# Attention scores by 64-row tiles, carried in PSUM from chunk to chunk, in turns of two chunks

## The chip, the core and the metric

The kernel runs on one core of a Trainium2 chip. TensorE multiplies matrices into PSUM, VectorE (DVE in the profile), ScalarE (ACT) and GpSimd (POOL) work on tiles, and SyncE (SP) issues the transfers between HBM and SBUF. The metric is device microseconds of one execution. Before the change three runs took 1882.86, 1883.38 and 1887.03 us, median 1883.38.

## The reference

One encoder layer runs on two sequences, "prompt" with 1024 tokens and "sample" with 2048, all in float32, 1024 channels wide. What matters here, cut from the reference:

```python
def hybrid_layer(x, mem, ...):
    h = rms_norm(x, norm_pre)
    z = jnp.einsum('btd,de->bte', h, w_in)
    u_pool, g_pool, q, k, v, g_attn, q_x, g_x = jnp.split(z, SPLITS, axis=-1)
    pool_out = multiscale_pool(u_pool, pool_w, pool_scale) * jax.nn.silu(g_pool)
    q = apply_rope(rms_norm(q.reshape(B, T, N_HEADS, HEAD_DIM), q_norm), cos, sin)
    k = apply_rope(rms_norm(k.reshape(B, T, N_KV_HEADS, HEAD_DIM), k_norm), cos, sin)
    attn_out = block_self_attention(q, k, v) * jax.nn.silu(g_attn)
    x_out = memory_attention(q_x, k_m, v_m) * jax.nn.silu(g_x)
    mix = jnp.concatenate([pool_out, attn_out, x_out], axis=-1)
    y = jnp.einsum('bte,ed->btd', mix, w_out)
    return x + rms_norm(y, norm_post)
```

Self-attention has 8 query heads of 64 dimensions and 2 key heads, so 4 query heads share one key head; it is not causal. Cross-attention has 4 heads over 256 memory tokens. Both are a softmax of scaled scores times values.

## The kernel before

**First stage.** The memory tokens, then blocks of 512 tokens, are normalised, transposed and multiplied by slices of `w_in`. For accuracy a float32 operand is split into a high part that the fast matmul format holds (`F32R`) and the rest, the low part (`split`), and a product is three matmuls: high by high, high by low, low by high. Queries and keys get norm and rotary positions, are transposed by TensorE (`heads_transposed`), split, and stored in HBM scratch: `DQ` and `DK` for self-attention, `DQX` and `DKM` for cross-attention, `DG` for the gates, `DV` for the values.

**Attention loop.** The queries are taken in pairs of two 128-query blocks (`Pair`, 256 queries; 8 pairs of the sample, then 4 of the prompt). A pair has three `Group`s: kind 0 and 1 are the two key heads with their four query heads, so 2 × 512 columns of queries; kind 2 is cross-attention. That makes 36 groups. A group runs over chunks of 128 keys: 16 in the sample, 8 in the prompt, 2 in cross-attention, 344 chunks in all.

The scores of a chunk stand with keys on the partitions. In `weights` two matmuls make them for each half `j` of the queries: `KA` has the high and the low part of the keys on its 128 partitions and meets the high part of the queries twice (`qa`); `KB` has the high part again and a 65th row of ones, and meets the low part of the queries and a 65th row with the negated maximum (`qb`). ScalarE takes the exponential of 512 columns from PSUM into `P`. `sums` adds the `P` of all chunks into `z`; in the sample VectorE adds one half and GpSimd the other (`CUT`), in the prompt VectorE adds all. `values` multiplies `P` by `V` in plain float32, two heads side by side in 64 columns of the array each, four chunks at a time (`RUN`). `totals` sums `z` over the keys, `inverse` takes the reciprocal and spreads it over 64 rows by way of HBM (`rows`, `gz`), `take` multiplies by the gate, and `mix_out` with `store_mix` multiplies by the inverse total and splits the result into `mix`.

The negated maximum comes from a look ahead: `largest` computes scores with queries on the partitions into a tile `N` of 1024 columns (two matmuls, two tiles in turn), and VectorE reduces it to one number per query. After a group's last look `shift` transposes these numbers and writes them to the row of `qb` in four small transfers.

**The order of work.** TensorE, ScalarE, VectorE and GpSimd run in the order in which the program is written; the transfers of SP are placed by the planner. The loop has one slot per chunk; work that belongs to a later slot is put in a list with `at` and issued by `due`. In a slot come the scores of half 0, the sums of the chunk before, one look, due work, the scores of half 1, pieces of the output projection (`piece`, three matmuls of 512 columns each) of an earlier pair, and work due at the half slot (`END`), where the values stand. `looks` is filled backward so that a group's last look stands at least `LEAD` = 4 slots ahead of its first. 20 looks are done beside the last matmuls of the first stage (`look_ahead`). PSUM in the loop holds two tiles `N` (two banks each), two `S` (one bank), `acc` and `py`.

## Time and profile before

| | |
|---|---|
| runs | 1882.86, 1883.38, 1887.03 us |
| profiled execution: span from first to last instruction | 1878.7 us |
| its own time outside the span | not recorded; the median of the runs is 4.7 us above the span |
| TensorE clock granted, mean | 0.994 |
| first scores of the loop, last values | 699.1 us, 1837.7 us |

The profile is one execution. Its busy time of TensorE counts overlapping matmuls once, and their modelled ends reach past the start of the next one, so the cost of a matmul is better read from the distance of two starts. In the lines of groups the shape `128*64` of a matmul is rows by columns of the weights, then comes rows by columns of what streams past; behind the bar stand the busy time, the mean in ns, and the idle time before with what ended it. `N`, `S`, `acc`, `py` are the tiles named above.

### The profile page before, as it was taken

The numbers are of one execution on the slowest core, as the hardware profiler recorded it, in microseconds if no ns is written. First come the engines' busy times: TensorE is split into PE (matmuls) and PEld (weight loads), VectorE is DVE, ScalarE is ACT, GpSimd is POOL, SyncE is SP. The second block draws the span as 40 slices with busy tenths as digits, with TensorE's granted clock in tenths as the row PEclk, the third lists the DMA queues.
The fourth block names the chain that finished last, engine by engine and source line by source line (L and its number), as shares of the span: only waits on it lengthen the run. The fifth ranks groups of instructions, "written<-read, shape, count | busy, mean of one in ns | idle before, by whom it ended". The sixth has DMA issues, their size and how long they took to land. (4 is left out here: it accounts for less than half of the span.)

```text
span 1878.7 us, 23531 instructions
## 1 busy us (share of the span) xinstructions
PE 1813.4 (97%) x8520; PEld 1279.4 (68%) x8520; DVE 1135.6 (60%) x1312; ACT 696.8 (37%) x1266; POOL 846.5 (45%) x748
## 2 busy tenths in 40 slices
PE   7999999999999999999999999999999999999997
PEld 6888888988988884465564656556465655565564
DVE  7745145431544168867768576776858576757744
ACT  5523234222422115444435344443434343333331
POOL 3655016520446007845638374563837452413311
PEclk9999999999999999999999999999999999999998
DMA  7634454254434926212122221212222153223211
GB/s 244 201 113 120 108 162 132 73 154 116 121 99 114 216 65 173 73 27 79 48 79 62 68 62 29 80 45 79 63 68 63 51 137 78 96 85 96 87 43 62
DMA packets 148485, 181.83 MB, mean 97 GB/s; under 512 B 21504, under 2 KB 118416, under 8 KB 148368
## 3 DMA queue, kind: packets, MB, share of 16 engines
q1 hardware_dynamic: 148368, 180.33, 33.9%
q8 instruction: 67, 1.10, 0.3%
q14 instruction: 50, 0.41, 0.1%
HBM read 126.50 MB, written 53.62 MB: 96 GB/s over the span
## 5 line engine op out<-in xcount | busy, mean ns | idle before, releaser
L227 ACT ACTIVATE P<-S 128x512 f32<-128x512 f32 x688 | 399.3, 598 | 555.5 <-PE S L220 430.8
L194 DVE TENSOR_REDUCE nb<-N 128x1 f32<-128x1024 f32 x256 | 311.7, 1218 | 239.8 <-PE N L191 239.0
L239 POOL TENSOR_TENSOR z<-z,P 128x512 f32<-128x512 f32 x224 | 318.4, 1421 | 222.5 <-ACT P L227 217.4
L252 PE MATMUL acc<-P,V 128*64 128x512 f32 (+1 forms) x1472 | 319.4, 576 | 0.5
L220 PE MATMUL S<-qa,KA 128*128 128x512 f32 x640 | 274.6, 429 | 9.7 <-ACT P L227 9.7
L63 POOL TENSOR_TENSOR rs<-rs,mhalf 128x1 f32<-128x1 f32 (+2 forms) x100 | 101.0, 1013 | 401.8 <-DVE rs L61 401.8
L240 DVE TENSOR_TENSOR z<-z,P 128x512 f32<-128x512 f32 (+1 forms) x272 | 271.0, 996 | 13.1 <-ACT P L227 12.9
L220 PE MATMUL S<-qb,KB 65*128 65x512 f32 x640 | 254.0, 397 | 0.0
L550 PE MATMUL pz<-hT_hi,w_hi 128*128 128x512 f32 x592 | 233.1, 394 | 1.3 <-ACT vmst L808 0.8
L552 PE MATMUL pz<-hT_hi,w_lo 128*128 128x512 f32 x592 | 232.1, 392 | 0.5 <-DVE w_lo L69 0.5
L551 PE MATMUL pz<-hT_lo,w_hi 128*128 128x512 f32 x592 | 232.3, 392 | 0.0
L191 PE MATMUL N<-KA,qa 128*128 128x512 f32 x640 | 207.5, 405 | 17.9 <-DVE rz L272 11.2
L252 PEld LDWEIGHTS acc<-P,V 128*64 128x64 f32 x1472 | 98.3, 138 | 178.7 <-issue 169.6
L220 PEld LDWEIGHTS S<-qa,KA 128*128 128x128 f32 x640 | 120.4, 188 | 143.9 <-issue 72.6
L194 DVE TENSOR_REDUCE top<-N 128x1 f32<-128x1024 f32 (+1 forms) x88 | 107.0, 1219 | 94.3 <-PE N L191 74.5
L191 PEld LDWEIGHTS N<-KA,qa 128*128 128x128 f32 x640 | 116.6, 191 | 60.9 <-DVE nb L194 21.9
L550 PE MATMUL pz<-w_hi,hT_hi 128*128 128x384 f32 (+1 forms) x416 | 140.2, 338 | 0.9 <-ACT hT_hi L68 0.8
L551 PE MATMUL pz<-w_lo,hT_hi 128*128 128x384 f32 (+1 forms) x416 | 139.4, 335 | 0.8 <-DVE w_lo L69 0.8
L552 PE MATMUL pz<-w_hi,hT_lo 128*128 128x384 f32 (+1 forms) x416 | 139.7, 338 | 0.0
L359 PE MATMUL py<-wo_hi,mix 128*128 128x512 f32 x352 | 137.7, 391 | 0.0
L360 PE MATMUL py<-wo_lo,mix 128*128 128x512 f32 x352 | 137.7, 391 | 0.0
L361 PE MATMUL py<-wo_hi,mix 128*128 128x512 f32 x352 | 137.4, 390 | 0.0
(120 smaller groups left out, 2479.5 us busy)
## 6 DMA issues: line engine op xcount, KB each, us to landing
wraw<-w_in SPq DMA_DIRECT2D x15, 1536.0 KB
dg<-gst SPq DMA_DIRECT2D x48, 256.0 KB
qa<-dq SPq DMA_DIRECT2D x48, 256.0 KB
gz<-rows SPq DMA_DIRECT2D x72, 128.0 KB
x<-x_sample SPq DMA_DIRECT2D x16, 512.0 KB
xr<-x_sample SPq DMA_DIRECT2D x16, 512.0 KB
y_sample<-xr SPq DMA_DIRECT2D x16, 512.0 KB
dq<-qst SPq DMA_DIRECT2D x96, 64.0 KB
```

Source lines behind the costliest of these rows:

```text
L191: nc.tensor.matmul(S[:, 512 * b:512 * b + 512], lhsT=q, rhs=KA[self.kind][:, k:k + 512], start=True, stop=True)
L194: nc.vector.tensor_reduce(out=out, in_=S, axis=AX.X, op=ALU.max, negate=True)
L220: nc.tensor.matmul(S, lhsT=K[self.kind][rows_, keys], rhs=q, start=n == 0, stop=n == 1)
L227: nc.scalar.activation(out=self.P[k][:, j], in_=S, func=AF.Exp)
L239: nc.gpsimd.tensor_tensor(out=z[:, :cut], in0=a[:, :cut], in1=P[:, :cut], op=ALU.add)
L240: nc.vector.tensor_tensor(out=z[:, cut:], in0=a[:, cut:], in1=P[:, cut:], op=ALU.add)
L252: nc.tensor.matmul(self.acc[64 * j:64 * j + 64, x], lhsT=v, rhs=P[:, j, x], start=(k, i) == (0, 0), stop=k == self.chunks - 1, skip_group_ ...
L359: nc.tensor.matmul(ps, lhsT=mh, rhs=wo_hi[:, c, cols], start=first, stop=False)
L360: nc.tensor.matmul(ps, lhsT=mh, rhs=wo_lo[:, c, cols], start=False, stop=False)
L550: nc.tensor.matmul(ps, lhsT=sh, rhs=mh, start=c == 0, stop=False)
L551: nc.tensor.matmul(ps, lhsT=sh, rhs=ml, start=False, stop=False)
L552: nc.tensor.matmul(ps, lhsT=sl, rhs=mh, start=False, stop=c == n - 1)
```

## The change

**Scores.** Keys and queries are laid out so that one half of the query heads has partitions 0 to 63 and the other 64 to 127. A matmul now contracts over 64 rows and the two halves stand side by side, each into its own PSUM bank of an `S` tile of 1024 columns. Two `S` tiles are used in turn, and a chunk's scores are not started afresh: the first two chunks of a group begin with a matmul of ones by a tile that holds the negated maxima (`rows`), and every chunk adds the product of the queries with the difference between its keys and those two chunks earlier. The first stage makes these differences and stores their high and low part (`DH`, `DL`), and the high part of the keys themselves for the looks (`KH`). Three products are added: high difference by high query, high by low, low by high. Cross-attention has keys of its own in both chunks and no carrying. The exponential takes 1024 columns at once.

**Looks.** A look covers 512 keys for two heads of 128 queries, by 64 rows, with the high part of the keys alone. It uses one tile `N` in the loop instead of two. The maxima of the parts are joined by a reduction; the shift goes out in eight small transfers, four for each half.

**Turns.** The loop advances by turns of two chunks: a look, the scores of both, a look, then totals and inverse of a finished group, projection, and the values of the turn before. `LEAD` is one turn.

**Rest.** `totals` uses the bank of `acc`. `inverse` transposes the totals, takes 8 reciprocals per row and spreads and transposes them back. The gate tile takes the gated product, with four buffers. The splits into `mix` are due when the tile `mix` of the pair before is free (`pair.free`), apart from the multiplication that makes their input. `P` has five buffers instead of six.

```diff
-    DK = [scratch(f"dk{s}", [2, 2, 64, T]) for s, (_, T) in enumerate(SEQS)]
+    DK = [scratch(f"dk{s}", [2, 3, 64, T]) for s, (_, T) in enumerate(SEQS)]
...
-        for a in range(0, SEQS[s][1], 1024):
-            nc.sync.dma_start(out=t[kind][h:h + 64, a:a + 1024].bitcast(F32), in_=DK[s][kind][hl, :, a:a + 1024])
+        for h in range(2):
+            for a in range(0, SEQS[s][1], 1024):
+                nc.sync.dma_start(out=tiles[kind][64 * h:64 * h + 64, a:a + 1024].bitcast(F32),
+                                  in_=DK[s][kind][which, :, a:a + 1024])
...
-            self.parts = 1 if kind == 2 else T // 1024
+            self.parts = 1 if kind == 2 else T // 512
             self.pieces = [(0, j) for j in range(2)] if kind == 2 else \
-                [(a, lane) for a in range(self.parts) for lane in range(8)]
-            self.P = {}
+                [(a, lane) for a in range(self.parts) for lane in range(4)]
+            self.P, self.S = {}, {}
...
-            self.gate = dbl.tile([128, 2, 2, 128], F32, name="gate", tag="gate")
+            self.gate = dbl.tile([128, 2, 2, 128], F32, name="gate", tag="gate", bufs=4)
...
-                q = self.qa[:, lane // 4, 128 * (lane % 4):128 * (lane % 4) + 128]
-                for b in range(2):
-                    k = 1024 * a + 512 * b
-                    nc.tensor.matmul(S[:, 512 * b:512 * b + 512], lhsT=q,
-                                     rhs=KA[self.kind][:, k:k + 512], start=True, stop=True)
-                out = self.nb[:, a, lane:lane + 1] if self.parts > 1 else self.top[:, lane:lane + 1]
+                for j in range(2):
+                    h = slice(64 * j, 64 * j + 64)
+                    nc.tensor.matmul(S[:, 512 * j:512 * j + 512],
+                                     lhsT=self.q[h, 0, 128 * lane:128 * lane + 128],
+                                     rhs=KH[self.kind][h, 512 * a:512 * a + 512], start=True, stop=True)
+                S = S.rearrange("p (j k) -> p j k", j=2)
+                out = self.nb[:, a].rearrange("p (j i) -> p j i", j=2)[:, :, lane]
...
             if self.parts > 1:
-                nc.vector.tensor_tensor(out=self.top[:, 0:8], in0=self.nb[:, 0], in1=self.nb[:, 1],
-                                        op=ALU.min)
-            self.qb = early.tile([128, 2, 512], F32R, name="qb", tag="qb", bufs=3)
-            load_K(self.s, self.kind, KB, 0, 0)
-            self.load_q(self.qb[0:64], 1)
+                nc.vector.tensor_reduce(out=self.top[:, 0:8], in_=self.nb.rearrange("p a i -> p i a"),
+                                        axis=AX.X, op=ALU.min)
+                load_K(self.s, self.kind, DH, 1)
+                load_K(self.s, self.kind, DL, 2)
             r = lanes_to_rows(self.top, "top")
-            row = self.qb[64:65].rearrange("o j (l b r) -> o (j l) b r", b=4, r=32)
-            for b in range(4):
-                nc.sync.dma_start(out=row[:, :, b].bitcast(F32), in_=r[32 * b:32 * b + 8])
-
-
-        def weights(self, k, j):
-            if j == 0:
-                self.P[k] = dbl.tile([128, 2, 512], F32, name="P", tag="P", bufs=6)
-            S = pss.tile([128, 512], F32, name="S", tag="S")
+            for j in range(2):
+                row = self.rows[64 * j:64 * j + 1].rearrange("o (i b r) -> o i b r", b=4, r=32)
+                for b in range(4):
+                    nc.sync.dma_start(out=row[:, :, b].bitcast(F32), in_=r[32 * b + 4 * j:32 * b + 4 * j + 4])
+
+
+        def weights(self, k):
+            self.P[k] = dbl.tile([128, 2, 512], F32, name="P", tag="P", bufs=PBUFS)
+            halves = [(slice(64 * j, 64 * j + 64), 512 * j) for j in range(2)]
             keys = slice(128 * k, 128 * k + 128)
-            for n, (K, q) in enumerate(((KA, self.qa[:, j]), (KB, self.qb[0:65, j]))):
-                rows_ = slice(0, 128 if n == 0 else 65)
-                if self.kind < 2:
-                    nc.tensor.matmul(S, lhsT=K[self.kind][rows_, keys], rhs=q, start=n == 0, stop=n == 1)
-                    continue
-                for i in range(2):
-                    x = slice(256 * i, 256 * i + 256)
-                    nc.tensor.matmul(S[:, x], lhsT=K[2][rows_, i, j, keys], rhs=q[:, x],
-                                     start=(n, i) == (0, 0), stop=(n, i) == (1, 1),
-                                     skip_group_check=True)
-            nc.scalar.activation(out=self.P[k][:, j], in_=S, func=AF.Exp)
+            if k < 2:
+                self.S[k] = pss.tile([128, 1024], F32, name="S", tag="S")
+                for h, at in halves:
+                    nc.tensor.matmul(self.S[k][:, at:at + 512], lhsT=ones_r[h], rhs=self.rows[h],
+                                     start=True, stop=False, skip_group_check=True)
+            S = self.S[k % 2]
+            for n, (kx, qx) in enumerate(((0, 0), (0, 1), (1, 0))):
+                for i in range(2 if self.kind == 2 else 1):
+                    x, w = (256 * i, 256) if self.kind == 2 else (0, 512)
+                    for h, at in halves:
+                        K = K2[0][h, i, kx, keys] if self.kind == 2 else (DH, DL)[kx][self.kind][h, keys]
+                        nc.tensor.matmul(S[:, at + x:at + x + w], lhsT=K, rhs=self.q[h, qx, x:x + w],
+                                         start=False, stop=n == 2, skip_group_check=True)
+            nc.scalar.activation(out=self.P[k].rearrange("p j q -> p (j q)"), in_=S, func=AF.Exp)
...
-            self.zt = psn.tile([128, 1024], F32, name="N", tag="N")
+            self.zt = psa.tile([128, 512], F32, name="acc", tag="acc")
...
-            self.o = dbl.tile([128, 512], F32, name="o", tag="o")
-            nc.vector.tensor_tensor(out=self.o, in0=self.acc,
-                                    in1=self.gate.rearrange("p i t q -> p (i t q)"), op=ALU.mult)
+            self.o = self.gate.rearrange("p i t q -> p (i t q)")
+            nc.vector.tensor_tensor(out=self.o, in0=self.acc, in1=self.o, op=ALU.mult)
 
         def inverse(self):
 
-            r = dbl.tile([128, 256], F32, name="rz", tag="rz", bufs=1)
-            nc.vector.reciprocal(out=r, in_=self.zt[:, 0:256])
+            r = dbl.tile([128, 8, 32], F32, name="rz", tag="rz", bufs=1)
+            nc.vector.transpose(out=r.rearrange("p b r -> p (b r)"), in_=self.zt[:, 0:256])
+            one = dbl.tile([128, 8], F32, name="ro", tag="ro", bufs=1)
+            nc.vector.reciprocal(out=one, in_=r[:, :, 0])
+            nc.vector.tensor_copy(out=r, in_=one.unsqueeze(2).broadcast_to([128, 8, 32]))
+            self.gz = dbl.tile([128, 512], F32, name="gz", tag="gz")
+            back = self.gz[:, 0:256]
+            nc.vector.transpose(out=back, in_=r.rearrange("p b r -> p (b r)"))
             rows = dram.tile([4, 256], F32, name="rows", tag="rows", bufs=4)
-            nc.sync.dma_start(out=rows, in_=r[0:128:32])
-            self.gz = dbl.tile([128, 512], F32, name="gz", tag="gz")
+            nc.sync.dma_start(out=rows, in_=back[0:128:32])
...
-        hi, lo = [m[:, c:c + 2] for m in pair.mix]
-
         e = nc.vector if pair.last else nc.gpsimd
         e.tensor_tensor(out=a, in0=a, in1=b, op=ALU.mult)
-        at(slot + 1 + END, nc.scalar.copy, hi, a)
-        at(slot + 2, e.tensor_tensor, lo, a, hi.bitcast(F32), ALU.subtract)
+
+        def high():
+            nc.scalar.copy(out=pair.parts()[0][:, c:c + 2], in_=a)
+
+        def low():
+            hi, lo = [m[:, c:c + 2] for m in pair.parts()]
+            e.tensor_tensor(out=lo, in0=a, in1=hi.bitcast(F32), op=ALU.subtract)
+
+        free = max(slot, pair.free)
+        at(free + 0.4, high)
+        at(free + 0.6, low)
...
-    HOLD = (16, 26)
-    LEAD, RUN = 4, 4
+    HOLD = (12, 21)
+    LEAD, PBUFS = 1, 5
...
+        pair.free = 6 if pair is pairs[0] else first[pair.groups[0]] + HOLD[pair.s]
+        at(min(ends) + 2, pair.pool, min(ends) + 2)
         for g in pair.groups:
...
+            wait = first[g] + g.chunks // 2 + 2
+            at(wait + 0.6, g.mix_out, wait + 1, pair)
+        at(max(max(ends) + 5, pair.free + 1), open_fill, pair, max(max(ends) + 5, pair.free + 1))
+    value_runs, sums_at = {}, {}
     for g in groups:
...
+        n, c = first[g], g.chunks // 2
+        at(n + 0.2, g.load_late)
+        for k in range(c):
+            value_runs[n + k + 1] = g, [2 * k, 2 * k + 1]
+        at(n + c + 0.6, g.take)
+        sums_at[n + c + 1] = g
...
+        for _ in range(2):
+            able = [g for g in groups if left[g] and first[g] - LEAD > n]
+            if able:
+                looks.setdefault(n, []).insert(0, (able[0], left[able[0]].pop()))
...
+            if k == 0:
+                loads.setdefault(max(n - 2, -1), []).append(g)
...
+            if keys is not None:
+                old = steps[keys % 2]
+                d = pt[:, 1]
+                if keys > 1:
+                    d = ftwo.tile([128, 128], F32, name="kstep", tag="kstep")
+                    nc.vector.tensor_tensor(out=d, in0=pt[:, 1], in1=old, op=ALU.subtract)
+                split(o[:, 0, 2], o[:, 1, 2], d)
+                nc.scalar.copy(out=old, in_=pt[:, 1])
...
-                    store_heads(o, 1, DK[s][j][:, :, 128 * tt:128 * tt + 128], j)
+                    store_heads(o, 0, DQ[s, tt // 2, 1][j, :, :, tt % 2, 1], j)
+                    store_heads(o, 2, DK[s][j][1:3, :, keys].rearrange("x d t -> d x t"), j)
+                    nc.sync.dma_start(out=DK[s][j][0, :, keys], in_=o[64 * j:64 * j + 64, 0, 1].bitcast(F32))
...
+    psn = pool("psn2", 1, PSUM)
...
+        n = -(-len(fill) // max(1, until[0] - turn)) if fill else 0
+        for _ in range(n):
+            out, h, c, start, final = fill.pop(0)
+            out.piece(h, c, start, final)
...
+            for x in loads.get(turn, ()):
+                x.load()
+            due(turn)
+            look(turn)
+            if before:
+                before.sums(kb + 1)
+            due(turn + 0.2)
             if g:
...
+                g.weights(k)
+                g.weights(k + 1)
+            look(turn)
+            if turn in sums_at:
+                sums_at[turn].totals()
+                sums_at[turn].inverse()
             if g:
...
+                g.sums(k)
+            due(turn + 0.4)
+            pieces = project(turn)
+            if turn in sums_at or (fill and until[0] > turn):
+                next(pieces)
+            if turn in value_runs:
+                h, ks = value_runs[turn]
+                h.values(ks)
+            for _ in pieces:
+                pass
+            due(turn + 0.6)
+            turn += 1
```

More of the change, by code (lines that the diff above doesn't have):

```diff
@@ L299, in __init__ @@
             self.last = (s, p) == (0, SEQS[0][1] // 256 - 1)
+            self.mix = None
         def load_pool(self):
@@ L407, in encoder, with at, due @@
         groups += pair.groups
-    slots = [(g, k) for g in groups for k in range(g.chunks)]
+    turns = [(g, k) for g in groups for k in range(0, g.chunks, 2)]
     later = {}
-    END = 0.5
-    def at(slot, f, *args):
-        later.setdefault(slot, []).append((f, args))
-    def due(slot):
-        for f, args in later.pop(slot, ()):
+    def at(turn, f, *args):
+        later.setdefault(round(turn, 2), []).append((f, args))
+    def due(turn):
+        for f, args in later.pop(round(turn, 2), ()):
@@ L418, in due, with open_fill @@
             f(*args)
     first = {}
-    for n, (g, k) in enumerate(slots):
+    for n, (g, k) in enumerate(turns):
         first.setdefault(g, n)
     fill, until = [], [0]
-    def open_fill(pair, slot):
+    def open_fill(pair, turn):
         fill.extend(pair.todo())
         n = pairs.index(pair) + 1
-        until[0] = first[pairs[n].groups[0]] + HOLD[pairs[n].s] if n < len(pairs) else slot
+        until[0] = first[pairs[n].groups[0]] + HOLD[pairs[n].s] if n < len(pairs) else turn
     for pair in pairs:
-        ends = [first[g] + g.chunks - 1 for g in pair.groups]
+        ends = [first[g] + g.chunks // 2 - 1 for g in pair.groups]
@@ L439, in encoder @@
+        at(max(max(ends) + 5, pair.free + 1), open_fill, pair, max(max(ends) + 5, pair.free + 1))
+    value_runs, sums_at = {}, {}
     for g in groups:
-        n, c = first[g], g.chunks
-        at(n + END, g.load_late)
-        for k in range(0, c, RUN):
-            ks = list(range(k, min(k + RUN, c)))
-            at(n + ks[-1] + 1 + END, g.values, ks)
-        at(n + c + 1 + END, g.totals)
-        at(n + c + 2, g.take)
-        at(n + c + 2 + END, g.inverse)
+        n, c = first[g], g.chunks // 2
[4 more added lines that the diff above has]
+        sums_at[n + c + 1] = g
@@ new lines, in project @@
+    def project(turn):
+        n = -(-len(fill) // max(1, until[0] - turn)) if fill else 0
+        for _ in range(n):
+            out, h, c, start, final = fill.pop(0)
+            out.piece(h, c, start, final)
+            if final:
+                if h == 0 and not out.last:
+                    for m in sorted(later):
+                        for x in [x for x in later[m] if x[0].__name__ in ("square", "norm", "out")]:
+                            later[m].remove(x)
+                            x[0](*x[1])
+                out.half_out(h)
+                at(turn + 0.6, out.square, h)
+                if h == 1:
+                    at(turn + 1, out.norm)
+                    at(turn + 1.6, out.out)
+                yield
+        yield
```

180 lines of the change are left out of this document (74 added, 106 removed).

## The prediction

> **What bounds the kernel now.** I read the page first, then busy time by stage, then the order of matmuls on TensorE inside one stage.
>
> ```profile
> span 1878.7 us, 23531 instructions
> PE 1813.4 (97%) x8520; PEld 1279.4 (68%) x8520; DVE 1135.6 (60%) x1312; ACT 696.8 (37%) x1266; POOL 846.5 (45%) x748
> PE   7999999999999999999999999999999999999997
> DVE  7745145431544168867768576776858576757744
> ```
>
> TensorE is busy from end to end, and no other engine is near it. The stages, busy microseconds behind the length of each:
>
> ```profile
> 0.00:708.00 708.00, 691.10 (x3491) 601.53 (x3492) 325.75 (x479) 222.34 (x389) 263.94 (x357) 1.00 0.49 136
> 708.00:800.00 92.00, 84.87 (x355) 44.09 (x353) 76.98 (x74) 47.52 (x80) 76.56 (x46) 0.98 0.42 116
> 800.00:1600.00 800.00, 784.49 (x3539) 474.27 (x3540) 561.09 (x594) 333.68 (x615) 430.92 (x303) 1.00 0.23 66
> 1600.00:1838.00 238.00, 225.06 (x1021) 139.46 (x1021) 154.14 (x147) 88.00 (x172) 67.64 (x38) 0.98 0.28 85
> 1838.00:1879.00 41.00, 27.87 (x120) 20.08 (x116) 17.60 (x22) 5.32 (x13) 7.40 (x6) 0.88 0.12 45
> ```
>
> The first stage (projections) is nearly untouched by the change. The attention loop is its field; its first scores and its last values stand here:
>
> ```profile
> 699.11 0.40 PE L224 MATMUL S<-qa,KA 128*128 128x256 f32 x2
> ...
> 1837.70 3.65 PE L252 MATMUL acc<-P,V 128*64 128x512 f32 x16
> ```
>
> So the loop has 1837.7 − 699.1 = 1138.6 us for 344 slots, 3.31 each. A busy share says little of what a matmul costs, since each lasts longer than the distance to the next; the timeline of TensorE gives the distances:
>
> ```profile
> 1206.47 0.63 PE L191 MATMUL N<-KA,qa 128*128 128x512 f32 x2
> 1206.94 0.39 PE L220 MATMUL S<-qa,KA 128*128 128x512 f32 x1
> 1207.17 0.39 PE L220 MATMUL S<-qb,KB 65*128 65x512 f32 x1
> 1207.49 3.65 PE L252 MATMUL acc<-P,V 128*64 128x512 f32 x16
> 1211.08 0.50 PE L220 MATMUL S<-qa,KA 128*128 128x512 f32 x1
> 1211.41 0.40 PE L220 MATMUL S<-qb,KB 65*128 65x512 f32 x1
> 1211.66 0.63 PE L191 MATMUL N<-KA,qa 128*128 128x512 f32 x2
> ```
>
> From 1206.47 to 1207.17 three matmuls pass: 0.233 us each, the unit of what follows. The values (64 columns, two heads side by side) asked from their third pair on:
>
> ```profile
> 1208.40 2.74 PE L252 MATMUL acc<-P,V 128*64 128x512 f32 x12
> ```
>
> and by duration:
>
> ```profile
> L252 PE MATMUL acc<-P,V x16: 592/592/644, 1207.5 to 1210.6; 128*64 128x512 f32 x16
> ```
>
> Twelve instructions are six pairs; less the last one's 0.59, five distances take 2.15 us: 0.43 a pair. A pair is two instructions of 0.59 us passing in 0.43, so two tiles of the array do run at once, by columns. Changing shape costs: from 1207.17 to 1211.66 are 4.49 us for three full matmuls (0.70) and eight pairs (3.44); the remaining 0.35 is one change into the values and one out of them, 0.175 each.
>
> **The change, part by part.**
>
> *Scores.* A chunk now takes four full-height matmuls (two heads, two products); after, three pairs of 64 rows (the pairs for high key step by high query, high by low, low by high). That 64-row tiles run side by side is in no row of before. Bounds for a pair: 0.233 if it goes like one matmul, 0.466 if one follows the other. I take 0.233, by the value pairs as the nearest row. 344 × 4 × 0.233 = 320.6 becomes 344 × 3 × 0.233 = 240.5: **−80.1**. The first two chunks of each of 36 groups also load the shift by a pair of ones: 72 × 0.233 = **+16.8**.
>
> *Looks.* Each was two matmuls, is now one pair. 20 looks lay before the loop, 18 will: 324 × 2 × 0.233 = 151.0 becomes 326 × 0.233 = 76.0, **−75.0**.
>
> *Values, projection, totals* keep count and price; only their place moves.
>
> *Changes of shape.* Before: 92 runs of values (four chunks; two in the memory groups) and 36 totals, two changes each: 256 × 0.175 = 44.8. After, each of 172 turns goes from 64-row tiles to projection, to values, and back: three changes, two in some 33 turns without projection, and one more for each total: about 520 × 0.175 = 91.0, **+46.2**. A 64-row change has no row; between 0 and 0.2 us (the 0.09 ahead of the first value and 0.10 in the two gaps after the last), I take 0.175. [...] If going from 64 rows to full height were free, the sum would be about 30 us lower.
>
> Sum on TensorE: −80.1 + 16.8 − 75.0 + 46.2 = **−92**.
>
> *Exponential.* One instruction of 1024 per chunk for two of 512.
>
> ```profile
> L227 ACT ACTIVATE P<-S 128x512 f32<-128x512 f32 x682 | 396.0, 598 | 554.4 <-PE S L220 430.5 <-issue 72.9 <-POOL o L290 25.0
> ```
>
> ```profile
> PE S L220 <- ACT P L227: 9.7, 31, 0.8
> ```
>
> At most 2 × 0.60 per chunk, 2.4 a turn beside 5.5 of TensorE. The scores now wait for the exponential of two chunks back, a whole half turn old: **−9**, the 9.7 that TensorE waits.
>
> *VectorE and one look buffer.* In the loop two buffers of N become one; the second look of a turn needs the first's maximum read.
>
> ```profile
> L194 DVE TENSOR_REDUCE nb<-N 128x1 f32<-128x1024 f32 x235 | 286.2, 1218 | 197.9 <-PE N L191 197.1
> L240 DVE TENSOR_TENSOR z<-z,P 128x512 f32<-128x512 f32 x224 | 205.8, 919 | 3.1 <-ACT P L227 3.0
> L240 DVE TENSOR_TENSOR z<-z,P 128x1024 f32<-128x1024 f32 x48 | 65.1, 1357 | 10.0 <-ACT P L227 9.9
> L272 DVE RECIPROCAL rz<-N 128x256 f32<-128x256 f32 x36 | 63.0, 1749 | 4.7 <-PE N L260 3.6 <-DMA rows<-rz 1.1
> L385 DVE SCALAR_TENSOR_TENSOR y<-y,rs,npost 128x1024 f32<-128x1024 f32 x22 | 31.4, 1427 | 3.3 <-POOL rs L63 3.3
> L266 DVE TENSOR_TENSOR o<-acc,gate 128x512 f32<-128x512 f32 x36 | 24.5, 682 | 3.8 <-POOL mix L418 3.8
> L128 DVE STREAM_TRANSPOSE rows<-top 128x32 f32<-128x32 f32 x34 | 7.2, 212 | 1.2
> ```
>
> A turn of the sample costs TensorE six score pairs and two looks (1.86), values (1.72), six projections (1.40), three changes (0.53): 5.5 us. VectorE: two maxima (2.44), two sums (1.84), and per group the gate (0.68) and the inverse. The new inverse is two transposes, a short reciprocal and a copy; at least three times 0.21, at most the 1.75 of the reciprocal that it replaces, I take 1.3. With outputs (1.43 per 128 rows) that is 0.65 a turn: 4.9 of 5.5. Within a turn, the first maximum ends at 0.4 + 1.22 = 1.6 us when VectorE is free, and TensorE asks for the buffer after 0.23 + 1.40 = 1.6: no wait with a free VectorE, up to a microsecond behind a gate or an output, and in the 21 first turns, without projection (4.1 on TensorE against some 4.9), always. Loss by looks: 0 to 100 us, I take 0.25 × 172 = 43. Now TensorE idles 7, 16 and 13 us in the three windows of the loop; less some changes of shape I call 30 of that waits of this kind: **+13**.
>
> *Group starts.* The shift now comes in eight small transfers, not four, and the last look stands one turn and a half ahead instead of four slots.
>
> ```profile
> 642.67 1.25 SPq L99 DMA_DIRECT2D KB<-dk  x2
> 760.17 0.56 SPq L274 DMA_DIRECT2D rows<-rz  x1
> 761.96 1.09 SPq L278 DMA_DIRECT2D gz<-rows  x2
> 1221.10 2.80 SPq L209 DMA_DIRECT2D qb<-rows  x4
> ```
>
> SP issues one in 0.70 us, so eight take 5.6; a landing is seen 1.23 us after its issue ended (760.73 to 761.96). From the last look: 0.4 to its end, 0.9 behind a sum, 1.22 maximum, 0.4 for minimum and transpose, 5.6, 1.2: 9.7 us. It has 3.6 us of its own turn, a turn of 5.8 and a look, 9.6. No slack: scores of the new group, and all of TensorE behind them, wait for whatever SP had queued ahead (an output's store, a gate). 0 to 2.5 us for each of 36, I take 0.6: **+22**.
>
> *Totals in the bank of acc.* Totals now wait for the gate product, and the next group's first values for the inverse's first transpose. Ahead of the totals lie two score blocks and two looks (1.9 us, over the 0.68), ahead of the values two projection pieces (1.4, over some 0.4 behind a maximum's 1.22): nothing. Without that cover it would be some 2 us for each of 36 groups, 72.
>
> *Key loads.* Each kind's steps are now two tiles in both halves: eight loads (2 MB) ahead of the shift in the sample, four in the prompt, for two now. At 0.62 us an issue that is 5.0 or 2.5 us late for four groups, less what is hidden: 0 to 15, I take **+10**.
>
> *First stage.* Three more copies of 128x128 on ScalarE and two on VectorE per 128 tokens, 48 more stores.
>
> ```profile
> L671 ACT COPY vst<-pz 128x128 f32<-128x128 f32 x24 | 6.4, 268 | 19.7 <-PE pz L552 12.1 <-DMA dv<-vst 5.4 <-issue 2.2
> ```
>
> 24 × 3 × 0.27 = 19 us on an engine busy 222 of 708; TensorE's 691 hide it. Uncovered they would cost those 19. With the looks' changes of shape in this stage I take **+2**. Late splits move instructions of equal count off full queues: nothing, covered by the same TensorE work.
>
> Sum: 1878.7 − 92 − 9 + 13 + 22 + 10 + 2 = 1824.7. The run's median, 1883.4, lies 4.7 above the span (start and end outside it), so **1829**.
>
> **Rivals.**
>
> *Pairs do not pass as one* (slower). One mechanism: the two 64-row tiles share something, so that a pair takes more than 0.233. The loop has 1032 + 72 + 326 = 1430 pairs; the gain of 54 us is gone at 0.233 + 54/1430 = 0.271 and at 0.466 the time is 1829 + 333 = 2162. For it: no row shows row tiles, and a pair needs two weight loads. Against: the value pairs, whose loads also come two by two, lose nothing. With only the weight load uncovered, the 0.10 by which 1211.08 to 1211.41 exceeds 0.233, it is 1829 + 143 = 1972. [...]
>
> *Late shifts or VectorE take it back.* All 36 starts at 2.5 us: +68, 1897; VectorE's loss at 100 instead of 43: +57, 1886. For it: no slack in either sum. Against: VectorE's average stays at 4.9 of 5.5.
>
> *Better than the sum.* 64-row changes free (−30), starts covered (−22), loads hidden (−10): 1767.
>
> **How the numbers follow.** Forecast 0.60, better 0.15, late shifts or VectorE 0.13, pairs apart 0.12. The range runs from 1767 to 1897 and leaves out the pairs rival's upper part and a little more below. A difference of 0.2% (3.8 us) is about what a measurement of this kernel can tell. Faster: 0.60 + 0.15 + a third of 0.13 = 0.80; same 0.04; slower 0.16.
>
> **What would show it.** Right: in the timeline, score pairs 0.23 apart, two starts within hundredths; looks likewise; three gaps of some 0.2 a turn; a turn of 5.8 us in the sample; VectorE at some 80% in the loop. Group starts: the wait of the ones matmul for the shift's transfers. Wrong: pairs at 0.3 or more, the looks waiting over half a microsecond a turn for VectorE, or waits of microseconds at group starts.

## The result and the profile after

| | time, us | ratio to before, 95% interval |
|---|---|---|
| before | 1883.14 median of 4 (1882.86 to 1887.03) | |
| after | 1823.99 median of 4 (1819.87 to 1825.72) | 0.9683 [0.9667, 0.9700] |
| forecast | 1829, range 1767 to 1897 | 0.971 |

The change makes the kernel 3.2% faster. The page of the kernel after, span, engines, TensorE's busy slices and its granted clock:

```profile
span 1823.9 us, 25529 instructions
PE 1740.7 (95%) x9400; PEld 1167.3 (64%) x9400; DVE 1144.1 (63%) x1472; ACT 656.0 (36%) x970; POOL 831.2 (46%) x748
PE   7999999999999998689999999999999999999997
PEclk9999999999999999799999999999999999999998
```

TensorE is still the busiest, but where before had nines from end to end there are now an 8, a 6 and an 8 in the slices that hold the start of the attention loop, and a 7 in the clock beside them. Busy time by stage of the kernel after (length of the stretch; then busy microseconds with counts of PE, PEld, DVE, ACT, POOL; then TensorE's clock, DMA share, GB/s):

```profile
0.00:700.00 700.00, 678.99 (x3399) 586.48 (x3400) 325.96 (x512) 226.40 (x427) 259.56 (x356) 0.99 0.49 138
...
708.00:800.00 92.00, 66.11 (x388) 33.55 (x388) 59.17 (x66) 38.30 (x41) 60.52 (x38) 0.89 0.50 146
800.00:1600.00 800.00, 783.27 (x4460) 415.66 (x4458) 617.34 (x717) 316.54 (x391) 449.98 (x317) 0.99 0.20 63
```

From 708 to 800 us TensorE is idle 25.9 us; before, in the same stretch, 7.1. In the quiet loop it is idle 16.7 of 800 us (before 15.5), and VectorE has gone from 561 to 617.

One turn of the sample, on TensorE, in the kernel after (start, length of the group, line, what it writes and reads, count):

```profile
1203.61 0.50 PE L186 MATMUL N<-KH,q 64*128 64x512 f32 x2
1203.94 0.63 PE L224 MATMUL S<-q,DH 64*128 64x512 f32 x4
1204.41 0.39 PE L224 MATMUL S<-q,DL 64*128 64x512 f32 x2
1204.64 0.63 PE L224 MATMUL S<-q,DH 64*128 64x512 f32 x4
1205.11 0.40 PE L224 MATMUL S<-q,DL 64*128 64x512 f32 x2
1205.43 0.49 PE L186 MATMUL N<-KH,q 64*128 64x512 f32 x2
1205.86 0.50 PE L373 MATMUL py<-wo_hi,mix 128*128 128x512 f32 x1
1206.19 0.39 PE L374 MATMUL py<-wo_lo,mix 128*128 128x512 f32 x1
...
1207.12 0.40 PE L375 MATMUL py<-wo_hi,mix 128*128 128x512 f32 x1
1207.45 1.94 PE L251 MATMUL acc<-P,V 128*64 128x512 f32 x8
1209.32 0.50 PE L186 MATMUL N<-KH,q 64*128 64x512 f32 x2
```

From 1203.94 to 1204.64 three score pairs pass: 0.233 us a pair, as one full-height matmul did. The turn lasts 1209.32 − 1203.61 = 5.71 us. The price of going from one shape to another is what the distances have over 0.233 a pair or matmul and 0.43 a pair of values: values to look 0.15 and on from the look to the scores, which have its shape, 0.10; look to projection and its first matmul 0.20 + 0.10; projection to values 0.10.

VectorE in the same turn of the kernel after, the maximum of the first look:

```profile
1204.15 1.23 DVE L191 TENSOR_REDUCE nb<-N 128x2 f32<-128x1024 f32 x1 [1.70 <-PE N L186]
```

It ends at 1205.38, and the second look starts at 1205.43: the one buffer of N is handed over with nothing to spare, although VectorE had stood idle for 1.70 us before.

**Where the time went.** I added up, from every matmul of the loop (first scores to last values), the distance to the next start, put it down to what the matmul was, and counted what a distance over 0.95 us has beyond 0.3 as a stop:

| loop, us | before | after | difference |
|---|---|---|---|
| scores, with the shift's pairs | 375.9 | 282.0 | −93.9 |
| looks | 163.7 | 122.8 | −40.9 |
| values | 312.5 | 324.6 | +12.1 |
| projection (1056 matmuls, then 1032) | 247.4 | 273.7 | +26.3 |
| totals | 19.9 | 19.9 | 0 |
| stops | 22.2 | 43.9 | +21.7 |
| sum | 1141.6 | 1067.0 | −74.6 |

The first scores start 13.7 us later than before (712.8 for 699.1), and what follows the start of the last values is 6.1 us longer (44.0 for 37.9). −74.6 + 13.7 + 6.1 = −54.8, the difference of the spans. My sum had −56, +2 and 0. Work that runs at half the clock (a granted 0.50, as from 1145.43 to 1148.82 us of the kernel after) is in its own line of the table; by the granted clock it costs some 7 us before and 15 after.

### The profile page after: what moved, and what is told of

Read it like the earlier page. It is cut to its first block, busy times and chain, and to the rows that moved or that the text cites. A ratio compares the mean times of both kernels' runs of the same rounds, so it can differ in the third digit from the quotient of the medians.

```text
span 1823.9 us, 25529 instructions
## 1 busy us (share of the span) xinstructions
PE 1740.7 (95%) x9400; PEld 1167.3 (64%) x9400; DVE 1144.1 (63%) x1472; ACT 656.0 (36%) x970; POOL 831.2 (46%) x748
## 4 chain that ended last, share of the span: by engine, by line
PE 80%; DVE 9%; issue 4%; DMA 3%; POOL 1%; SPq 1%; ACT 1%; DVEq 0%; ACTq 0%; POOLq 0%
PE acc L251 16%; PE pz L569 10%; PE pz L571 10%; PE pz L570 10%; PE S L224 9%; PE N L186 6%; PE py L373 6%; PE py L375 4%; PE py L374 4%; DVE nb L191 4%; DVE z L239 2%; PE S L216 1%; PE acc L259 1%; DVE gate L265 1%; PE pt L544 1%
## 5 line engine op out<-in xcount | busy, mean ns | idle before, releaser
L226 ACT ACTIVATE P<-S 128x1024 f32<-128x1024 f32 x344 | 334.6, 1023 | 567.8 <-PE S L224 294.0
L191 DVE TENSOR_REDUCE nb<-N 128x2 f32<-128x1024 f32 x320 | 391.0, 1222 | 166.0 <-PE N L186 165.1
L251 PE MATMUL acc<-P,V 128*64 128x512 f32 (+1 forms) x1472 | 336.6, 581 | 3.9 <-DVE rz L270 3.9
L239 DVE TENSOR_TENSOR z<-z,P 128x512 f32<-128x512 f32 (+1 forms) x272 | 265.5, 976 | 16.7 <-ACT P L226 16.5
L224 PE MATMUL S<-q,DH 64*128 64x512 f32 x1280 | 206.1, 395 | 10.3 <-ACT P L226 10.3
L186 PEld LDWEIGHTS N<-KH,q 64*128 64x128 f32 x640 | 60.7, 184 | 196.3 <-DVE nb L191 95.4
L186 PE MATMUL N<-KH,q 64*128 64x512 f32 x640 | 157.9, 488 | 25.2 <-DVE nb L191 21.6
L373 PE MATMUL py<-wo_hi,mix 128*128 128x512 f32 x352 | 156.3, 444 | 0.0
L224 PEld LDWEIGHTS S<-q,DH 64*128 64x128 f32 x1280 | 122.3, 186 | 34.9 <-ACT P L226 10.6
L375 PE MATMUL py<-wo_hi,mix 128*128 128x512 f32 x352 | 141.0, 401 | 0.0
L69 DVE TENSOR_TENSOR w_lo<-wraw,w_hi 128x3072 fp32r<-128x3072 f32 (+2 forms) x21 | 67.8, 3228 | 107.9 <-ACT w_hi L68 107.5
L569 PEld LDWEIGHTS pz<-hT_hi,w_hi 128*128 128x128 f32 x592 | 111.9, 189 | 30.6 <-issue 4.5
```

The source lines that it names most:

```text
L186: nc.tensor.matmul(S[:, 512 * j:512 * j + 512], lhsT=self.q[h, 0, 128 * lane:128 * lane + 128], rhs=KH[self.kind][h, 512 * a:512 * a + 512 ...
L191: nc.vector.tensor_reduce(out=out, in_=S, axis=AX.X, op=ALU.max, negate=True)
L224: nc.tensor.matmul(S[:, at + x:at + x + w], lhsT=K, rhs=self.q[h, qx, x:x + w], start=False, stop=n == 2, skip_group_check=True)
L226: nc.scalar.activation(out=self.P[k].rearrange("p j q -> p (j q)"), in_=S, func=AF.Exp)
L239: nc.vector.tensor_tensor(out=z[:, cut:], in0=a[:, cut:], in1=P[:, cut:], op=ALU.add)
L251: nc.tensor.matmul(self.acc[64 * j:64 * j + 64, x], lhsT=v, rhs=P[:, j, x], start=(k, i) == (0, 0), stop=k == self.chunks - 1, skip_group_ ...
```

## The experiments

Each ratio is to the kernel before, run beside it on the same chip. The kernel after has 0.9683 [0.9667, 0.9700].

| label | edit | median, us | ratio |
|---|---|---|---|
| e2_heads_apart | one head's score matmuls, then the other's (two runs) | 1826.18 | 0.9701 [0.9681, 0.9722] |
| e4_third_twice | third score pair twice | 1860.74 | 0.9881 [0.9866, 0.9897] |
| e5_no_third | third score pair left out | 1812.89 | 0.9630 [0.9610, 0.9649] |
| e3_lead_two | looks two turns ahead | 1823.30 | 0.9677 [0.9660, 0.9693] |
| e7_before_run_two | kernel before, values by two chunks | 1919.13 | 1.0198 [1.0182, 1.0213] |
| e1_w_out_pace | output weights at half the pace | 1825.27 | 0.9688 [0.9672, 0.9703] |
| e8_first_mix_late | first group's mix four turns later | 1813.92 | 0.9634 [0.9613, 0.9655] |
| e6_qst_three | three buffers for the transposed heads | 1823.72 | 0.9686 [0.9669, 0.9702] |
| e9_one_key_store | one store of keys per head, not two | 1820.62 | 0.9671 [0.9657, 0.9685] |
| e10_late_mix_early_ones | e8, and the ones set early | 1815.86 | 0.9648 [0.9635, 0.9661] |
| e11_late_mix_one_store | e10 and e9 | 1808.57 | 0.9605 [0.9586, 0.9624] |
| e13_output_later | e11, output scaling 0.8 turns later | 1797.34 | 0.9538 [0.9521, 0.9555] |

**Do the pairs need their order?**

```diff
-            for n, (kx, qx) in enumerate(((0, 0), (0, 1), (1, 0))):
...
-                    for h, at in halves:
+            for h, at in halves:
+                for n, (kx, qx) in enumerate(((0, 0), (0, 1), (1, 0))):
```

> The same score matmuls in another order: the three products of one half of the heads, then the three of the other, so a matmul and its neighbour in the other 64 rows no longer stand next to each other. Theory: TensorE starts matmuls in the order of the program, and two run at once only when the next one is in the other rows. Then a chunk takes five distances of 0.231 instead of three: 344 x 0.46 = 159 us more, less some 30 that the second look's wait gives back, 1950 to 1985 us. Rival: the two halves of the array run on their own, whatever the order: 1824 us. The gain then would not hang on the order in pairs.

Measured: 1826.2 us, no difference from the change. My theory, that heads written one after the other pass one after the other, fell. The timeline of this kernel, the scores of a chunk and the start of the next:

```profile
1203.21 0.63 PE L224 MATMUL S<-q,DH 64*128 64x512 f32 x4
1203.68 0.39 PE L224 MATMUL S<-q,DL 64*128 64x512 f32 x2
1203.91 0.63 PE L224 MATMUL S<-q,DH 64*128 64x512 f32 x4
```

In the written order each head's two DH are followed by its DL before the other head begins, and the trace shows the first head's and the second head's matmuls starting together all the same, 0 to 3 ns apart, 0.23 us from pair to pair. That fits two halves of rows that go forward each on its own, if the built program keeps the written order. The trace has starts and no program order, so it doesn't show that. One sign for it: behind the stop of 11 us at 744 the second head starts 10 ns after the first, where it is 3 in the kernel after.

**What bounds a turn?** Two runs around the score pairs, one with a pair more, one with a pair less.

```diff
-            for n, (kx, qx) in enumerate(((0, 0), (0, 1), (1, 0))):
+            for n, (kx, qx) in enumerate(((0, 0), (0, 1), (1, 0), (1, 0))):   # e4
+            for n, (kx, qx) in enumerate(((0, 0), (0, 1))):                   # e5
```

> The third product of every chunk (low part of the key steps by the high queries) is done twice, so it is added twice. 344 more pairs at 0.231 us are 79 us. If TensorE is the bound and nothing else waits inside a turn: 1903 us. Theory by the trace: in most turns the second look waits some 0.2 us for VectorE's maximum of the first, since one buffer serves both; 0.46 us more between them hides that: 1903 less 30 to 45, so 1858 to 1873 us. If VectorE or ScalarE set the pace: under 1840 us.

> The third product of every chunk is left out (low part of the key steps by the high queries). 344 pairs less at 0.231 us are 79 us. If TensorE's matmuls alone set the time: 1745 us. Theory: the two looks of a turn share one buffer, and the first maximum takes about 1.87 us from the start of its matmul to the freed buffer; the distance falls from 1.84 to 1.38 us, so most of the 79 us comes back as a wait of the second look: 1795 to 1822 us.

A pair is 344 × 0.231 = 79 us of TensorE. One more costs 37, one fewer saves 11. With one pair more, a turn:

```profile
1201.05 0.50 PE L186 MATMUL N<-KH,q 64*128 64x512 f32 x2
...
1203.26 0.40 PE L186 MATMUL N<-KH,q 64*128 64x512 f32 x2
1203.58 0.50 PE L373 MATMUL py<-wo_hi,mix 128*128 128x512 f32 x1
...
1207.04 0.50 PE L186 MATMUL N<-KH,q 64*128 64x512 f32 x2
```

With one pair less:

```profile
1203.76 0.50 PE L186 MATMUL N<-KH,q 64*128 64x512 f32 x2
...
1205.58 0.51 PE L186 MATMUL N<-KH,q 64*128 64x512 f32 x2 [0.39 <-DVE nb L191]
...
1209.48 0.50 PE L186 MATMUL N<-KH,q 64*128 64x512 f32 x2
```

With a pair less the second look still comes 1.82 us after the first, as in the kernel after, and the turn is 5.72 instead of 5.71: TensorE only waits. With a pair more the turn is 5.99, 0.28 longer for 0.46 of work, and the second look is followed by the projection after 0.32, not 0.43. So in the kernel after the second look waits 0.09 for the maximum, and its weights, whose load starts only with it at 1205.43, cost another 0.10, by 0.43 to the projection for 0.32. (Weight loads of looks wait for VectorE 112 times from 800 to 1600 us there, 24 times in the run with a pair more.) The look's round (look, maximum of 1.22 us, next look: 1.82) is the limit of that half of the turn; taking work from TensorE there gives nothing any more. From 800 to 1600 us the looks of the run with a pair less wait 61.7 us in all for VectorE (13.1 in the kernel after); its 11 us come from other turns; from which isn't settled. The 37 us of the run with a pair more are less than 172 × 0.28 = 48, since in the turn without projection the stop is shorter (1.6 us between two starts for 2.1) and work at half the clock costs some 8 us for 15.

**Do group starts cost what I gave them?**

```diff
-    LEAD, PBUFS = 1, 5
+    LEAD, PBUFS = 2, 5
```

> A group's last look stands two turns ahead of its first scores, not one, and all looks move with it. The prediction put 0.6 us of waiting on each of 36 group starts, 22 us: then 1802 us. The trace has only two waits at group starts, both in the first 70 us of the loop. Theory by the trace: eight transfers land just in time, later groups wait for nothing: 1824 within 4 us, or down to 1816 if the stop of 9 us after 764.6 goes.

0.9677 against 0.9683: no difference. TensorE's wait for the shift behind 764 us falls from 7.7 to 0.6 us, but it stands 6.6 us for GpSimd's sums at 773 instead. The waits of TensorE between 800 and 1785 us of the kernel after (total, times, longest):

```profile
PE N L186 <- DVE nb L191: 18.9, 14, 2.9
...
PE S L216 <- DMA rows<-rows: 0.4, 1, 0.4
```

From 800 us on the shift's transfers are waited for once, 0.4 us. My +22 was wrong.

**Changes of shape, in the kernel before.**

```diff
-    LEAD, RUN = 4, 4
+    LEAD, RUN = 4, 2
```

> The kernel before the change with values after every two chunks instead of four. It prices changes of shape by themselves: 80 runs more, two changes each of 0.175 us, 28 us: 1911 us if they lie on the path that sets the end. If TensorE would have waited there anyway: 1884 to 1890 us.

+36 us, above both forecasts, but most of it is a wait and not the price of shape changes. The first values of a group need the bank of `acc`, which the gate product `o` of the group before has to free. They now come too early for it:

```profile
PE acc L252 <- DVE o L266: 31.8, 19, 3.0
```

The kernel before has no such wait. Where scores precede values, the mean distance is 0.62 us for 0.32; without these 19 it is 0.32 here too. All of TensorE's waits together are 20 us longer and the half clock takes some 6 more, which leaves some 13 of the loop's 39 for 160 changes, an estimate, and less than the 28 of the forecast. So the run doesn't give the price; the timeline of the kernel after, above, does.

**The start of the loop.** The longest stop of the kernel after, on TensorE:

```profile
754.26 1.22 PE L224 MATMUL S<-q,DH 64*128 64x512 f32 x4 [10.27 <-ACT P L226]
...
771.07 0.76 PE L216 MATMUL S<-rows,ones_r 64*128 64x512 f32 x1 [5.98 <-DMA rows<-rows]
```

Followed back, through ScalarE, GpSimd and SP's queue (a fence each):

```profile
752.24 1.04 ACT L118 CAST wo_hi<-raw 128x1024 fp32r<-128x1024 f32 x1 [13.76 <-DMA raw<-w_out]
```

```profile
745.14 1.26 POOL L291 TENSOR_TENSOR gate<-gate,gz 128x512 f32<-128x512 f32 x1 [14.39 <-DMA gz<-rows]
```

```profile
718.63 2.53 SPq L99 DMA_DIRECT2D DH<-dk  x4
721.21 7.12 SPq L99 DMA_DIRECT2D DL<-dk  x4
...
738.46 0.53 SPq L278 DMA_DIRECT2D rows<-gz  x1
741.63 1.11 SPq L281 DMA_DIRECT2D gz<-rows  x2
748.73 0.35 SPq L114 DMA_DIRECT2D raw<-w_out  x1
```

The key steps take SP's queue for 9.7 us; the first group's inverse, ready on VectorE at 726.6, gets out behind them and eight other loads at 738.5 and is back at 745. GpSimd stands in front of its product for 14.4 us, and the splits of the output weights stand behind that product, the first at 746.4. A buffer of those weights comes free late, its load goes out at 748.7, ScalarE waits for it before the cast, and the exponentials that TensorE needs are behind the cast. Two runs tell the links apart. The first slows the output weights:

```diff
-        at(2 + c, load_w_out, c)
-        at(3 + c + 0.6, split_w_out, c)
+        at(2 + 2 * c, load_w_out, c)
+        at(4 + 2 * c + 0.6, split_w_out, c)
```

> The output weights are loaded every second turn and split two and a half turns after their load, instead of every turn and one and a half turns after it. The trace of the changed kernel has two stops of TensorE at the start of the loop, 10.8 us after 743.5 and 9 us after 764.6. Theory: GpSimd waits in order for a late spread of the first inverse total, so it frees the buffers of the output weights late, their next loads hold SP, and ScalarE waits in order for them, with the exponentials behind it. Then both stops shrink: 1824 - 10 to 18, so 1806 to 1814 us. Rival: the 2 MB of key steps themselves keep the data away, and the stops only move: 1820 to 1827 us.

The second takes the waiting product out of GpSimd's way:

```diff
-            wait = first[g] + g.chunks // 2 + 2
+            wait = first[g] + g.chunks // 2 + (6 if g is groups[0] else 2)
```

> The first group's product with its inverse total, which GpSimd does, stands four turns later. In the trace GpSimd stands 14.4 us before it, because the transfers that spread the total are queued behind 4 MB of keys and values, and then its sums and the splits of the output weights are late. Theory: that wait of GpSimd, in order, is what stops TensorE at 743.5 and 764.6 us. Without it: 1824 less 10 to 18, 1806 to 1814 us. Rival, after the slower pace of the output weights brought nothing: the transfers behind the keys are what is late whoever waits for them, and the stops move to the next one that needs a transfer: 1820 to 1827 us.

With slower weights the first stop shrinks from 10.8 to 2.0 us between two starts, but GpSimd still stands, the second stop grows to 7.8 and others come after it: 0.9688, nothing gained. With the later mix the long stops go, and 10 us with them (0.9634). The step at fault is the place of the first group's mix.

**The first stage.** The first suspect was the buffer of the transposed heads:

```diff
-            o = ftwo.tile([128, 2, 3, 128], F32R, name="qst", tag="qst")
+            o = ftwo.tile([128, 2, 3, 128], F32R, name="qst", tag="qst", bufs=3)
```

> Three buffers for the staging tile of queries and keys in the first stage, not two. The first scores come at 712.8 us, 13.7 later than before the change, where the prediction allowed 2. Theory: the tile now has more and later stores, and ScalarE waits for its buffer (4.0 us before the matmul stop of 2.6 us at 325.7): half of the loss returns, 1816 to 1820 us. Rival: the loss comes from SP, which issues 48 more stores ahead of the loads of x: 1822 to 1826 us.

No effect (first scores at 712.8 still). The next was SP's 48 additional stores; high and low steps of a head's keys go out in one again, the old number of stores:

```diff
-                    store_heads(o, 2, DK[s][j][1:3, :, keys].rearrange("x d t -> d x t"), j)
-                    nc.sync.dma_start(out=DK[s][j][0, :, keys], in_=o[64 * j:64 * j + 64, 0, 1].bitcast(F32))
+                    nc.sync.dma_start(out=DK[s][j][:, :, tt].rearrange("x d c t -> d x c t"),
+                                      in_=o[64 * j:64 * j + 64, :, 1:3].bitcast(F32))
```

> Question: what the changed kernel loses in the first stage (its first scores start at 712.8 us instead of 699.1; I had put +2). The change there adds 48 stores of keys on SP. Here the two key stores per head and 128 tokens are one again, with the same bytes but one step more; the loads read the same bytes in pieces of 512 bytes. If SP's issues are what delays the first stage (about 0.65 us for each of 48): first scores at 705 to 709 us and a time 4 to 8 us under 1824, ratio 0.964 to 0.967. If the loss is in the copies and products on ScalarE and VectorE: first scores stay at 712 to 713, ratio 0.967 to 0.970.

The first 700 us of this kernel, and after it of the kernel before:

```profile
0.00:700.00 700.00, 684.38 (x3436) 590.34 (x3437) 327.11 (x515) 226.60 (x428) 259.45 (x356) 1.00 0.51 140
```

```profile
0.00:700.00 700.00, 684.26 (x3450) 596.57 (x3450) 319.77 (x473) 217.31 (x382) 262.66 (x356) 1.00 0.49 136
```

TensorE is as busy again as before (684.4 and 684.3; the kernel after 679.0), with ScalarE's and VectorE's extra copies still in place. The first scores come at 704.5 us, 8.3 earlier, and the profiled span is 8.0 shorter. The medians differ by 3.4 only, within their intervals; in the next two runs, on one chip, the same store makes 7.3.

```diff
-    ones_r = own.tile([128, 128], F32R, name="ones_r")     # when the loop opens
+    ones_r = const.tile([128, 128], F32R, name="ones_r")   # at the kernel's start
```

> The first group's mix four turns later, as before (1813.9, ratio 0.963), and beside it the ones that load the shift are set at the kernel's start instead of when the attention loop opens (the first ones matmul waited some 2 us at 710 for them). If that wait is a wait of its own: 1812, ratio 0.9615 to 0.963. If another thing (the shift's rows, the first keys) ends just behind it: no change against 0.963.

> The two edits of the run before and the one key store together. If the store helps by itself, the gains add: 1805 to 1809, ratio 0.958 to 0.961. If not: 1811 to 1814, ratio 0.9615 to 0.9635, or up to 2 us more by the loads in shorter pieces.

The ones alone: 0.9648 against 0.9634 without, no gain. Their wait is gone and the first scores come at 710.2 us (712.0 in e8), but the first values now wait 2.3 us for their `V`. With the one store, 0.9605, below 0.9648 with intervals apart. So 8.3 of the 13.7 us in the first stage are SP's additional stores; whether their issue or their transfers isn't told apart.

**The stop in the turn without projection.** Once a pair, the kernel after stands as here, VectorE first, then TensorE:

```profile
1141.04 2.32 DVE L399 SCALAR_TENSOR_TENSOR y<-y,rs,npost 128x1024 f32<-128x1024 f32 x1
1143.28 1.21 DVE L191 TENSOR_REDUCE nb<-N 128x2 f32<-128x1024 f32 x1
```

```profile
1144.54 0.50 PE L186 MATMUL N<-KH,q 64*128 64x512 f32 x2 [1.70 <-DVE nb L191]
```

The scaling of a finished output is ahead of the maximum that the second look waits for, and takes 2.3 us. And the stop has an echo, in the granted clock (the number before the last two):

```profile
1144.00:1146.00 2.00, 1.46 (x5) 1.04 (x6) 2.00 (x3) 0.18 (x1) 2.00 (x2) 0.86 0.52 151
1146.00:1148.00 2.00, 2.00 (x6) 0.96 (x6) 2.00 (x2) 0.00 (x0) 2.00 (x3) 0.50 0.56 169
1148.00:1150.00 2.00, 2.00 (x10) 0.38 (x6) 0.01 (x1) 0.00 (x0) 2.00 (x1) 0.79 0.56 178
```

Work runs again from 1144.5, and from 1145.43 to 1148.82 at half the clock (0.50 granted): over the 8 us behind the stop 0.79, that is 1.7 us lost besides the 1.7 of the stop. The last run moves the scaling:

```diff
-                    at(turn + 1.6, out.out)
+                    at(turn + 2.4, out.out)
```

> The two edits and the one key store of the run before (1808.6, ratio 0.9605), and beside them the scaling of a finished output on VectorE stands 0.8 turns later in the written order, behind the maxima of the one turn per pair that has no projection, instead of ahead of them. In that turn the second look now stands 2.1 us (1.75 of them idle), eight times in the sample, and 3.2 us twice in the prompt; and behind each such stop the granted clock is 0.79 over the next 8 us in about half of the cases (1.7 us more). If the place of the scaling makes the stop: these stops fall under 1.2 us, the clock stays at 1.00 behind them, and the time is 12 to 22 us lower, 1787 to 1797, ratio 0.949 to 0.955. If VectorE is only out of time in that turn: the stop moves to the next look or stays, 1805 to 1812, ratio 0.959 to 0.962. Between the two, 1797 to 1805: the scaling now costs a look of a turn with projection about one microsecond.

0.9538 against 0.9605: 11 us less. (The eight stops of which the expectation speaks are six in the sample and two in the prompt.) The waits of TensorE between 800 and 1600 us, of the looks in the kernel without this edit (e11), then the longest in this one, and the window itself:

```profile
PE N L189 <- DVE nb L194: 15.3, 15, 2.9
```

```profile
PE N L181 <- DVE top L194: 4.4, 6, 1.1
PE S L219 <- DMA rows<-rows: 3.3, 7, 1.1
PE N L189 <- DVE nb L194: 1.9, 7, 0.7
```

```profile
800.00:1600.00 800.00, 787.20 (x4526) 421.19 (x4524) 618.30 (x723) 320.89 (x400) 454.52 (x316) 1.00 0.21 67
```

The stops of 2.1 and 3.2 us from start to start are 0.9 to 1.1, 1.4 in one, and the clock is 1.00 (0.99 in the kernel after). The looks wait 6.3 us for 15.3; what is left is mostly a look of cross-attention (`top`), 0.7 us once a pair, and new are 3.3 us for the shift. The time, 1797.3, lies just above what I gave for the place as the cause. This kernel beats both: 4.6% under before.

## Why the prediction was right, and where only its sum was

The forecast of 1829 against 1824 holds, and most of its mechanism, but one term that was much too high, the group starts, hides two that were too low, the key loads and the first stage: 22 + 10 + 2 = 34 forecast, some 0.4 + 18.8 + 13.7 = 33 measured. That these cancel is luck.

- **Pairs pass as one: right.** 0.233 from score pair to score pair. A look that doesn't wait has 0.32 to the projection behind it (e4): the same price, and 0.09 for the change of shape. The rival with 0.271 as its break-even is out, in both its forms: the loads of a score pair's two weights (1204.18 us in the turn above, for the pair at 1204.41) run while the pair ahead does, and the pairs stay 0.233 apart.
- **Changes of shape: right in size.** No row of before had a change between 64 rows and full height; it costs 0.20 from look to projection (less the 0.10 of the waiting look's weights: 0.09 is left in e4, where the look doesn't wait). Projection to values costs 0.10, values to look and scores 0.25. So a turn has 0.55 for the 0.53 of the sum.
- **Quiet work of the loop: right.** By 0.233 a pair or matmul and 0.43 a pair of values, scores, looks, values and projection come to 320.6 + 151.0 + 296 + 246 before and 257.3 + 76.0 + 296 + 240.5 after. What the table has beyond these is 85.9 before and 133.3 after: +47 for shape changes, exponentials and looks. With the looks' stops, which the table has apart, that is 53, where the sum had 46 − 9 + 13 = 50; some 8 of the 53 are the half clock behind stops, which no term had. The 9 for the exponential came: from 800 us on no wait for it is left.
- **Looks and one buffer: right, by another route.** I expected no wait with a free VectorE; it is 0.09 in a quiet turn and its weights 0.10, and 1.7 us in the turn without projection. That this turn would always lose was in the prediction, and so was a wait behind an output; that both meet in one turn wasn't, nor the clock.
- **Group starts: the step that failed, +22 for nearly 0.** The working had the shift landing in 9.7 us with 9.6 to spare and took "no slack" for a loss. It lands in time: the chain to its end was right, but what SP had queued ahead costs nothing outside the loop's first groups (0.4 us from 800 us on).
- **Key loads: +10, and it is more, by another route.** Three stops of TensorE from 743 to 774 us make 18.8 us. The eight loads were counted as lateness of the shift; what they delayed first is the first group's inverse, and with it GpSimd, the output weights, ScalarE. The working has no term for an engine that waits in order behind these loads; the nearest it has is "Late splits move instructions of equal count off full queues: nothing", and 10 us came back with one group's mix (e8). The other stops in the table's 43.9 us are looks that wait for VectorE, 20.9 (15.5 before, most of them for the reciprocal, which then sat in a tile `N`), and values that wait for the totals' bank, 4.2.
- **Totals in the bank of acc: nothing, and it is 4.2.** All three stops lie between 723 and 823 us; later the cover that I gave holds but for one wait of 0.8 us.
- **First stage: +2, and it is +13.7.** TensorE does hide the copies, as I said; I named the 48 stores and gave them no price. 8.3 us are theirs (e9), some 2 the late setting of the ones (e10); the remaining 3 to 4 aren't settled by a run.
- **Tail: 0, and it is +6.1.** 24 projection matmuls have gone from the loop to behind it (1056 and 1032 in the table): 24 × 0.233 = 5.6, a move, not a loss; it makes the loop's gain look larger by as much. That these two are the same was worked out, not tested.
- **The new inverse: +1.3, and it is more.** The groups of VectorE from 800 to 1600 us of the kernel after:

```profile
L273 DVE COPY rz<-ro 128x256 f32<-128x256 f32 x25 | 19.2, 768 | 0.9
...
L276 DVE STREAM_TRANSPOSE gz<-rz 128x256 f32<-128x256 f32 x25 | 11.1, 445 | 0.9
L270 DVE STREAM_TRANSPOSE rz<-acc 128x256 f32<-128x256 f32 x25 | 11.0, 440 | 2.2 <-PE acc L259 2.2
```

  These three are 1.65 us, and with the small reciprocal of 0.20 they are 1.85, about as long as the old one of 1.75; it has saved VectorE nothing.

## What to carry to other kernels

When work is taken off the engine that bounds, look for the shortest round through a single buffer (here look, maximum, look: 1.82 us): from there on work that was saved came back as a wait, as the run with a pair less shows (79 us of matmuls fewer, 11 us of time). Price a DMA that is added to a full queue by what stands behind it in that queue, not by itself, and an engine that waits in order by everything queued behind the wait: one group's product four turns later gave 10 us, 48 stores fewer 7. A stop of TensorE should be counted with the half clock behind it: here 1.7 us more behind six of eight stops.

## What was not expected of the hardware

- Pairs of 64-row matmuls start side by side in both written orders: with one head's matmuls written ahead of the other's, 809 of 960 pairs still start within 5 ns of each other (796 in the kernel after), and the time is the same (1826.2 and 1824.0). That the built program keeps the written order is not shown.
- Behind a stop with 1.7 us of idle TensorE the granted clock was halved for some 3.4 us (0.50 from 1145.43 to 1148.82 us; 0.86, 0.50 and 0.79 in three windows of 2 us). In the kernel after, the 8 us behind its eight stops of 1.7 to 2.9 us from 900 us on have 0.79 six times and 1.00 twice, some 10 us in all; in the kernel with one store (e11) 0.79 or 0.80 only three times of eight. Why like stops differ is not shown: 1.7 us idle gave 0.79 at 1247 us and 1.00 at 1348, and 2.9 us gave 1.00 at 1611 and 0.79 at 1678.
- In the 10.8 us stop the clock falls some 2 us after the last matmul and stays at 0.50 to 0.57 from 746 to 760 us, through the first 5.5 us in which TensorE works again: this stop cost more than its length, by some 2.7 us.
